# Second-layer attention scores: two matmuls of 128 rows and one of 32 in place of three of 96 rows, and another order of the steps

## Chip, core and metric

The kernel runs on one core of a Trainium2 chip. The metric is the device time of one execution in microseconds. Engines are named as in the profile: PE (matrix multiplication; PEld its weight loads), DVE (vector), ACT (scalar, activations), POOL (general purpose), SP (issues the DMAs).

## What is computed

The reference is a backbone of two layers over 1024 latent tokens and 256 context tokens, in float32. The change lies in the second layer, multi-head latent attention. Each of 16 heads has queries and keys of 64 numbers made by projections ("nope") and 32 with rotary positions, which all heads share on the key side:

```python
def mla_keys_values(kv_a, k_pe, kv_norm, w_kvb, row, col):
    kv = (rms_norm(kv_a, kv_norm) @ w_kvb).reshape(B_, L, C_HEADS, C_NOPE + C_V)
    k_nope, v = kv[..., :C_NOPE], kv[..., C_NOPE:]
    k = jnp.concatenate([k_nope, jnp.broadcast_to(k_pe, (B_, L, C_HEADS, C_ROPE))], axis=-1)

def one(qblk):
    s = jnp.einsum('bqhd,bkhd->bhqk', qblk, k).astype(jnp.float32) * scale
    p = jax.nn.softmax(s, axis=-1).astype(v.dtype)
    return jnp.einsum('bhqk,bkhd->bqhd', p, v)
```

The queries are the 1024 latent tokens; the keys are all 1280 tokens.

## The kernel before, in words

Float32 products that need accuracy are made from two parts: a "high" part, the number rounded to the matmul's float32r format, and a "low" part, the rest. A product is the sum of high x high, high x low and low x high; `mm3` (L98) issues the three for the projections, and the function `scores` (L1201) does so for the scores. `hi` (L85) makes a high part by a cast, `lo` (L94) a low part by a subtraction.

`layer1_attention` (L1174) walks over 64 units: 8 pairs of heads, 4 groups of 256 queries, 2 heads. A unit has 256 queries of one head, as two blocks j of 128 queries, against 1280 keys. PSUM has eight banks: `s0` and `s1` take two each (the scores of a block j against 1024 keys), `sx` one (both blocks against the 256 context keys), `tm` has two buffers of one bank that transposes and projections take in turn, and `acc` one. `s0`, `s1` and `sx` have one buffer: the next unit's scores wait until the exponents have read them.

Inside `manual_schedule` the order of the instructions of PE, ACT, DVE and POOL is the order of the program, and that is written out by hand in `ORDER1` (L43), a list of steps that every unit n goes through:

- S0 S1 (block 0, keys 0 to 511 and 512 to 1023), S2 S3 (block 1), S4 (both blocks, context keys): `scores` on PE.
- X0 X1 X2: `maxima` on DVE; P0 P1: `peak`, a small DVE operation on them; E0 E1 (1024 keys) and E2 E3 (256): `exponent` on ACT.
- T0 to T4: `turn`, four transposes each of the previous unit's probabilities on PE and a copy out of `tm`, on the engine that `TURNS` (L45) names for each (V is DVE, A is ACT). T0 T1 are of block 0, T2 T3 of block 1, T4 of the context keys.
- A0: `av`, the product with the values, half of a pair of units' in each unit. I, U, C: the sums' inverses, their spreading (U is two PE transposes in odd units) and the gating of a finished pair.
- B and R: `prep_q`, in even units, the queries of the group that the unit after next starts with. B is the projection on PE, R what follows: casts and subtractions into `qh` and `ql`, with the rotary part loaded from DRAM by SP into `pe` and put into rows 64 to 95.
- D and L: a step each of `prep_v` ("value step") or `prep_pair` ("key step"), by `VALUES` and `PAIR` (L41). A key step's D is a projection on PE into a `tm` bank (512, 512 and 256 keys for a pair), its L two ACT casts and two DVE subtractions, one of each for a head, that empty that bank into `kring`.

`kring` holds the keys of the present pair of heads and the next; `kpe` (L1086) puts the rotary keys into its rows 64 to 95. SP has no order of its own by hand: its DMAs stand in the scheduler's order and are issued in turn.

The code that the change touches:

Of the kernel before, what the change touches and what calls it, by code (L numbers as in the profile page):

```python
# [41 lines left out]
WQ = 'VGG'  # L42
ORDER1 = 'S0 S1 T0 T1 I C X0 S4 S2 X2 P0 T2 T3 E0 E2 S3 T4 D X1 P1 L E3 E1 A0 U B R'.split()  # L43
AVS = ((0, 5),), ((5, 10),)
TURNS = 'VAAVA'  # L45
KPE = {3: [0], 5: [1]}
KPEE = "AV"
ORDER0 = 'S0 S1 D Q M S2 S3 A1 D D A2 P HV HG S4 U D A3 X I F'.split()
# [5 lines left out]
class Kernel:  # L54
# [887 lines left out]
    def layer1_in(self):  # L942
# [6 lines left out]
        self.kvl = lp.tile([P, T], F32R, name="kvl")  # L949
        self.pk = lp.tile([P, T], F32, name="pk")  # L950
        qn = lp.tile([P, 2], F32, name="qn")
        kn = lp.tile([P, 1], F32, name="kn")
        gp = self.pool(self.es_h1, "g1", bufs=2, side="right")
        es_r = ExitStack()
        rp = self.pool(es_r, "r1", bufs=2, side="right")
# [129 lines left out]

    def kpe(self, par, heads=range(2)):  # L1086

        for e in heads:
            kh, kl = self.kring[par][e]
            if par == 0:  # L1090
                self.hi("A", kh[64:96], self.pk[64:96])
                self.lo("V", kl[64:96], self.pk[64:96], kh[64:96])
            else:
                for to, v in zip((kh, kl), self.kring[0][e]):
                    self.hi(KPEE[to is kl], to[64:96], v[64:96].bitcast(F32))

# [32 lines left out]
    def prep_pair(self, hp):  # L1129
# [9 lines left out]
        for g0, gn in GROUPS:  # L1139
            ps = self.project(w, self.split(kvh, kvl), g0, gn)  # L1140
            yield
            c = slice(g0, g0 + gn)
            src = [ps[64 * e:64 * e + 64] for e in range(2)]
            for e in range(2):
                nc.scalar.copy(ring[e][0][0:64, c], src[e])
            for e in range(2):
                nc.vector.tensor_tensor(ring[e][1][0:64, c], src[e], ring[e][0][0:64, c].bitcast(F32), op=ALU.subtract)
            yield

    def prep_q(self, hp, qg):  # L1150

        nc = self.nc
        pool = self.qpool[qg % len(self.qpool)]
        cols = slice(qg * self.QG, (qg + 1) * self.QG)
        pe = self.t(self.c1, [P, 2, self.QG], F32, "pe", bufs=2)
        nc.sync.dma_start(pe[64:96], self.pe_d[64 * hp:64 * hp + 64, cols].rearrange("(e p) c -> p e c", e=2))
        tp = self.bank()
        w = self.wq[hp]
        for k in range(2):
            self.mm3(tp[:, 0:self.QG], *w[k], self.qnh[:, k, cols], self.qnl[:, k, cols], k == 0, k == 1)  # L1160
        yield
        qh = self.t(pool, [P, 2, self.QG], F32R, "qh", bufs=1)
        ql = self.t(pool, [P, 2, self.QG], F32R, "ql", bufs=1)
        src = [tp[64 * e:64 * e + 64, 0:self.QG] for e in range(2)]
        for e in range(2):
            nc.scalar.copy(qh[0:64, e], src[e])  # L1166
        for e in range(2):
            nc.vector.tensor_tensor(ql[0:64, e], src[e], qh[0:64, e].bitcast(F32), op=ALU.subtract)  # L1168
        self.hi("A", qh[64:96], pe[64:96])
        self.lo(WQ[2], ql[64:96], pe[64:96], qh[64:96])  # L1170
        self.pq[(hp, qg)] = [(qh[:, e], ql[:, e]) for e in range(2)]
        yield

    def layer1_attention(self):  # L1174
# [98 lines left out]
        def inverses(m):  # L1273

            t = totals.pop(m)
            nc.vector.tensor_tensor(t[:, 2], t[:, 0], t[:, 1], op=ALU.add)
            spread[m] = v = self.t(c2, [P, 2, 2, 64], F32, "spread", bufs=2)
            nc.vector.reciprocal(t[:, 2], t[:, 2])
# [43 lines left out]
        with self.tc.manual_schedule(engines={E.PE, E.Activation, E.DVE, E.Pool}):  # L1322
            for n in range(N + 3):
                odd = n % 2
                for op in ORDER1:
                    o, a = op[0], int(op[1:] or 0)
                    if o in "SXPE":
                        if n < N:
                            {"S": scores, "X": maxima, "P": peak, "E": exponent}[o](n, a)
                    elif o == "T":  # L1330
                        if 1 <= n <= N:
# [247 lines left out]
```

## Time and profile before

| | |
|---|---|
| runs | median 1504.61 us of 3 (1503.4 to 1506.65) |
| profiled execution | its own time 1504.3 us, its span 1502.5 us |
| PE busy | 1439.6 us, 96% of the span |
| DVE, ACT, POOL busy | 879.5, 735.9, 397.4 us |
| granted PE clock | 0.994 of full speed |
| first score matmul of the second layer | starts at 805.6 us |
| last unit's first score matmul | starts at 1389.4 us |

The span runs from the first to the last instruction. "Busy" is time in which an engine has an instruction under way; consecutive matmuls overlap in these records, so their durations add up to more than their share of the time, and the distance between starts tells the pace.

### The profile page before, as it was taken

What the parts mean: (1) busy time and instruction counts of PE and PEld (TensorE: products, weight loads), DVE (VectorE), ACT (ScalarE), POOL (GpSimd) and SP (SyncE); (2) the same over time, 40 slices, a digit from 0 to 9 for tenths busy, and PEclk for the clock granted to TensorE, in tenths of its full rate; (3) what the DMA queues carried; (4) which work ended last, traced back from release to release, by engine and by line L of the source; (5) the groups of instructions that cost most, each with busy time, mean ns of one, the idle gap of its engine ahead of it and who ended that gap; (6) DMA issues with size and microseconds to landing.
All of it is one profiled execution on the core that took longest, in us unless ns stands there. A gap on an engine that the chain in (4) does not pass through costs nothing.

```text
span 1502.5 us, 23133 instructions
## 1 busy us (share of the span) xinstructions
PE 1439.6 (96%) x8849; PEld 1132.6 (75%) x8849; DVE 879.5 (59%) x1690; ACT 735.9 (49%) x1563; POOL 397.4 (26%) x351
## 2 busy tenths in 40 slices
PE   5999999999999799999998999999999999999998
PEld 3766899777666478879887777777777777776786
DVE  5582124356667877543745766676667666766454
ACT  4422310145567635443435766666666666676321
POOL 4243233223556533232470110011001100124100
PEclk9999999999999999999999999999999999999999
DMA  8557401222214646321231000000000000212241
GB/s 329 230 219 272 136 29 29 85 81 85 72 39 155 188 123 191 130 76 57 71 127 39 24 24 15 25 24 24 15 25 24 24 15 22 71 46 81 96 144 71
DMA packets 83783, 132.64 MB, mean 88 GB/s; under 512 B 7552, under 2 KB 59976, under 8 KB 80600
## 3 DMA queue, kind: packets, MB, share of 16 engines
q1 hardware_dynamic: 83528, 130.91, 25.9%
q8 instruction: 69, 1.13, 0.3%
q14 instruction: 42, 0.34, 0.1%
q10 hardware_dynamic: 144, 0.26, 0.0%
HBM read 99.59 MB, written 31.56 MB: 87 GB/s over the span
## 4 chain that ended last, share of the span: by engine, by line
PE 75%; DVE 9%; ACT 5%; issue 4%; DMA 4%; POOL 2%; SPq 0%; POOLq 0%; DVEq 0%; ACTq 0%
PE acc L1270 9%; PE tm L1252 7%; PE s L100 7%; PE s L101 7%; PE s L102 7%; PE b L100 5%; PE b L101 4%; PE b L102 4%; PE s L1215 3%; PE s L1216 3%; PE s L1217 3%; PE tm L100 2%; PE acc L774 2%; DVE peak L1227 2%; ACT prob L1242 2%
## 5 line engine op out<-in xcount | busy, mean ns | idle before, releaser
L1259 ACT COPY pt<-tm 128x512 f32<-128x512 f32 x192 | 112.4, 585 | 165.7 <-PE tm L1252 165.7
L1252 PE MATMUL tm<-ident,prob 128*128 128x128 f32 x1280 | 178.3, 273 | 7.8 <-ACT pt L1259 2.1
L1252 PEld LDWEIGHTS tm<-ident,prob 128*128 128x128 f32 x1280 | 150.8, 140 | 42.0 <-PE tm L1252 9.5
L1242 ACT ACTIVATE prob<-s,peak 128x1024 f32<-128x1024 f32 x128 | 143.3, 1120 | 38.0 <-DVE peak L1231 29.6
L1227 DVE TENSOR_REDUCE peak<-s 128x1 f32<-128x1024 f32 x128 | 155.0, 1211 | 1.8 <-PE s L1217 1.7
L1270 PE MATMUL acc<-pt,v 128*64 128x256 f32 x1280 | 152.0, 384 | 0.0
L96 POOL TENSOR_TENSOR ql<-pe,qh 32x512 fp32r<-32x512 f32 x32 | 40.7, 1271 | 413.2 <-ACT qh L88 386.2
L1261 DVE COPY pt<-tm 128x512 f32<-128x512 f32 x128 | 87.8, 686 | 79.4 <-PE tm L1252 77.4
L96 POOL TENSOR_TENSOR w_lo<-raw,w_hi 128x512 fp32r<-128x512 f32 (+1 forms) x60 | 74.9, 1261 | 199.0 <-DVE w_hi L90 98.5
L1270 PEld LDWEIGHTS acc<-pt,v 128*64 128x64 f32 x1280 | 86.3, 136 | 49.7 <-issue 9.6
L1215 PE MATMUL s<-kh,qh 96*128 96x512 f32 x256 | 109.2, 426 | 2.5 <-DVE raw L186 1.5
L1216 PE MATMUL s<-kl,qh 96*128 96x512 f32 x256 | 100.9, 394 | 0.0
L1217 PE MATMUL s<-kh,ql 96*128 96x512 f32 x256 | 100.8, 394 | 0.0
L1168 DVE TENSOR_TENSOR ql<-tm,qh 64x256 fp32r<-64x256 f32 x62 | 26.1, 421 | 83.7 <-ACT qh L1166 83.3
L100 PE MATMUL b<-h,yh 128*128 128x512 f32 x160 | 63.8, 399 | 3.7 <-ACT yh L88 2.7
L100 PE MATMUL s<-h,w_hi 128*128 128x512 f32 x160 | 63.9, 412 | 2.2 <-ACT qk L380 2.2
L101 PE MATMUL s<-h,w_hi 128*128 128x512 f32 x160 | 63.7, 398 | 0.3 <-DVE rs_v L125 0.3
L101 PE MATMUL b<-h,yh 128*128 128x512 f32 x160 | 63.3, 395 | 0.0
L102 PE MATMUL s<-h,w_lo 128*128 128x512 f32 x160 | 63.0, 395 | 0.0
L102 PE MATMUL b<-h,yl 128*128 128x512 f32 x160 | 62.5, 391 | 0.0
L1242 ACT ACTIVATE prob<-sx,peak 128x256 f32<-128x256 f32 x128 | 61.0, 477 | 0.6
L1217 PEld LDWEIGHTS s<-kh,ql 96*128 96x128 f32 x256 | 48.0, 188 | 11.2
(469 smaller groups left out, 3733.7 us busy)
## 6 DMA issues: line engine op xcount, KB each, us to landing
wa<-in_w_ada_dram SPq DMA_DIRECT2D x16, 1024.0 KB, 9.1
x<-in_xs_dram SPq DMA_DIRECT2D x20, 512.0 KB, 5.6
raw<-in_w_dram SPq DMA_DIRECT2D x17, 512.0 KB, 3.6
wa<-in_w_adag_dram SPq DMA_DIRECT2D x8, 1024.0 KB, 5.9
raw<-in_w_out_dram SPq DMA_DIRECT2D x10, 512.0 KB, 3.9
yf<-y_d SPq DMA_DIRECT2D x10, 512.0 KB, 5.6
x_d<-x SPq DMA_DIRECT2D x8, 512.0 KB, 4.5
raw<-in_w1g_dram SPq DMA_DIRECT2D x8, 512.0 KB, 3.4
```

Of the source, the lines that this page charges most:

```text
L96: e.tensor_tensor(lo, src, hi.bitcast(F32), op=ALU.subtract)
L100: mm(out, lhsT=ah, rhs=bh, start=start, stop=False)
L101: mm(out, lhsT=ah, rhs=bl, start=False, stop=False)
L102: mm(out, lhsT=al, rhs=bh, start=False, stop=stop)
L1215: mm(o, lhsT=qh[0:96, q], rhs=kh[0:96, k0:k1], start=True, stop=False)
L1216: mm(o, lhsT=qh[0:96, q], rhs=kl[0:96, k0:k1], start=False, stop=False)
L1217: mm(o, lhsT=ql[0:96, q], rhs=kh[0:96, k0:k1], start=False, stop=True)
L1227: nc.vector.reduce_max(m[:, 0, a:a + 1], banks[n, a], axis=AX.X)
L1242: nc.scalar.activation(probs[n][j][:, TL:T] if c else probs[n][j][:, 0:TL], src, AF.Exp, bias=peaks[n][:, 2, j:j + 1], scale=scale, accum_ ...
L1252: nc.tensor.transpose(tp[:, o * P:(o + 1) * P], probs[n][j][:, k * P:(k + 1) * P], self.ident)
L1259: nc.scalar.copy(dst, src)
L1270: mm(accs[m][64 * e:64 * e + 64, 0:QG], lhsT=self.v4[hp // 2][:, kt, vc:vc + 64], rhs=pts[2 * m + e][:, kt], start=kt == 0, stop=kt == NT - 1)
```

## The change

Scores: the third matmul of each bank of 512 keys goes. The operands are packed anew so that two matmuls have 128 rows: `qa` holds high and low nope queries (64 + 64 rows) against the high nope keys, which now stand in `ka` twice; `qb` holds the high nope queries, the high rotary queries and the low rotary queries against the low nope keys and the high rotary keys twice. What is left is high rotary queries x low rotary keys, 32 rows. `qc` and `kc` hold these four times over, in rows 0, 32, 64 and 96, and `rotary` (step K) issues one matmul of 32 rows for each of the four banks of `s0` and `s1`, each from another group of 32 rows. For S4 a third matmul of 128 rows stays, with `kz`, in which the three spare copies are multiplied by 0.

The order: S2, S3 and K move ahead of X0; D and L move behind the products; B moves ahead of them; R stands right after E2. T3's copy goes to ACT and T4's to DVE. Copies and casts: `prep_pair` casts each high part twice, `prep_q` loads `pe` with four DMAs in place of one and gives POOL four operations in place of one (`WQ[2]` was G: POOL), `kpe` changes accordingly. `pe` and `spread` have one buffer in place of two, and `pk` moves to another pool.

```diff
-ORDER1 = 'S0 S1 T0 T1 I C X0 S4 S2 X2 P0 T2 T3 E0 E2 S3 T4 D X1 P1 L E3 E1 A0 U B R'.split()
+ORDER1 = 'S0 S1 T0 T1 I C S2 S3 K X0 T2 S4 T3 X2 P0 E0 B X1 P1 E2 R A0 E1 T4 D E3 U L'.split()
-TURNS = 'VAAVA'
+TURNS = 'VAAAV'
...
+        self.kc = k1.tile([P, T], F32R, name="kc")
+        self.kz = k1.tile([P, TC], F32R, name="kz")
...
+        first = self.kring[0][0][1]
         for e in heads:
-            kh, kl = self.kring[par][e]
-            if par == 0:
-                self.hi("A", kh[64:96], self.pk[64:96])
-                self.lo("V", kl[64:96], self.pk[64:96], kh[64:96])
-            else:
-                for to, v in zip((kh, kl), self.kring[0][e]):
-                    self.hi(KPEE[to is kl], to[64:96], v[64:96].bitcast(F32))
+            kb = self.kring[par][e][1]
+            if par or e:
+                self.hi("A", kb[64:128], first[64:128].bitcast(F32))
+                continue
+            for r in (64, 96):
+                self.hi("A", kb[r:r + 32], self.pk[64:96])
+            self.lo("V", self.kc[64:96], self.pk[64:96], kb[64:96])
+            for r in (0, 32, 96):
+                self.nc.vector.tensor_copy(self.kc[r:r + 32], self.kc[64:96].bitcast(F32))
...
             for e in range(2):
-                nc.scalar.copy(ring[e][0][0:64, c], src[e])
+                for r in (0, 64):
+                    nc.scalar.copy(ring[e][0][r:r + 64, c], src[e])
...
-        pe = self.t(self.c1, [P, 2, self.QG], F32, "pe", bufs=2)
-        nc.sync.dma_start(pe[64:96], self.pe_d[64 * hp:64 * hp + 64, cols].rearrange("(e p) c -> p e c", e=2))
+        pe = self.t(self.c1, [P, 2, self.QG], F32, "pe", bufs=1)
+        for r in range(0, P, 32):
+            nc.sync.dma_start(pe[r:r + 32], self.pe_d[64 * hp:64 * hp + 64, cols].rearrange("(e p) c -> p e c", e=2))
...
         for e in range(2):
-            nc.scalar.copy(qh[0:64, e], src[e])
+            nc.scalar.copy(qa[0:64, e], src[e])
         for e in range(2):
-            nc.vector.tensor_tensor(ql[0:64, e], src[e], qh[0:64, e].bitcast(F32), op=ALU.subtract)
-        self.hi("A", qh[64:96], pe[64:96])
-        self.lo(WQ[2], ql[64:96], pe[64:96], qh[64:96])
+            nc.vector.tensor_tensor(qa[64:128, e], src[e], qa[0:64, e].bitcast(F32), op=ALU.subtract)
+        self.hi("G", qc, pe)
+        self.lo("G", qb[96:128], pe[96:128], qc[96:128])
+        self.hi("G", qb[64:96], pe[64:96])
+        self.hi("G", qb[0:64], qa[0:64].bitcast(F32))
...
-                mm(o, lhsT=qh[0:96, q], rhs=kh[0:96, k0:k1], start=True, stop=False)
-                mm(o, lhsT=qh[0:96, q], rhs=kl[0:96, k0:k1], start=False, stop=False)
-                mm(o, lhsT=ql[0:96, q], rhs=kh[0:96, k0:k1], start=False, stop=True)
+                mm(o, lhsT=qa[:, q], rhs=ka[:, k0:k1], start=True, stop=False)
+                mm(o, lhsT=qb[:, q], rhs=kb[:, k0:k1], start=False, stop=False)
+                if a == 4:
+                    mm(o, lhsT=qc[:, q], rhs=self.kz, start=False, stop=True)
+
+        def rotary(n):
+            hp, qg, e = units[n]
+            qc = self.pq[(hp, qg)][e][2]
+            for g in range(4):
+                j, h = divmod(g, 2)
+                r = slice(32 * g, 32 * g + 32)
+                mm(banks[n, j][:, h * 512:(h + 1) * 512], lhsT=qc[r, j * P:(j + 1) * P],
+                   rhs=self.kc[r, h * 512:(h + 1) * 512], start=False, stop=True)
```

Three places of the order, all in the same odd unit, one with a key step. PE from the end of S1 on, before: S1, T0 T1 (each row of four transposes), S4 (its first row), S2, T2 T3. The numbers behind names tell tiles apart; rows of the changed kernel have its own line numbers.

```order
L1215 MATMUL s0_1346_8180<-kh11_7346,qh_1305_7974 128x512
L1216 MATMUL s0_1346_8180<-kl11_7347,qh_1305_7974 128x512
L1217 MATMUL s0_1346_8180<-kh11_7346,ql_1306_7975 128x512
L1252 MATMUL tm_1348_8188<-ident_69,prob_1331_8122 128x128 x4
L1252 MATMUL tm_1349_8194<-ident_69,prob_1331_8122 128x128 x4
L1215 MATMUL sx_1352_8206<-kh11_7346,qh_1305_7974 128x256
...
L1215 MATMUL s1_1353_8213<-kh11_7346,qh_1305_7974 128x512
L1216 MATMUL s1_1353_8213<-kl11_7347,qh_1305_7974 128x512
L1217 MATMUL s1_1353_8213<-kh11_7346,ql_1306_7975 128x512
L1252 MATMUL tm_1354_8219<-ident_69,prob_1332_8123 128x128 x4
L1252 MATMUL tm_1355_8225<-ident_69,prob_1332_8123 128x128 x4
```

The same place with the change: S1, T0 T1, S2 (S3 repeats its rows), K (two rows of two matmuls), T2, S4 (its first two rows), T3.

```order
L1227 MATMUL s0_1353_8234<-kh11_7366,qa_1306_7991 128x512
L1228 MATMUL s0_1353_8234<-kl11_7367,qb_1307_7992 128x512
L1275 MATMUL tm_1355_8240<-ident_69,prob_1337_8173 128x128 x4
L1275 MATMUL tm_1356_8246<-ident_69,prob_1337_8173 128x128 x4
L1227 MATMUL s1_1358_8256<-kh11_7366,qa_1306_7991 128x512
L1228 MATMUL s1_1358_8256<-kl11_7367,qb_1307_7992 128x512
...
L1239 MATMUL s0_1353_8234<-kc_7095,qc_1308_7993 128x512 x2
L1239 MATMUL s1_1358_8256<-kc_7095,qc_1308_7993 128x512 x2
L1275 MATMUL tm_1360_8267<-ident_69,prob_1338_8174 128x128 x4
L1227 MATMUL sx_1361_8273<-kh11_7366,qa_1306_7991 128x256
L1228 MATMUL sx_1361_8273<-kl11_7367,qb_1307_7992 128x256
...
L1275 MATMUL tm_1362_8280<-ident_69,prob_1338_8174 128x128 x4
```

S2 and S3 with K now stand between T1 and T2, and S4 between T2 and T3; each bank has two rows where it had three.

PE at the end of that unit, before: T4's last transpose, the three matmuls of the key step D (`kvh` and `kvl` with `w_hi` and `w_lo`, into a `tm` bank), the products (twenty records in the trace, ten rows here, one shown), U, and S0 of the next unit.

```order
L1252 MATMUL tm_1358_8238<-ident_69,prob_1332_8123 128x128
L100 MATMUL tm_1359_8244<-kvh_6005,w_hi_1337_8142 128x512
L101 MATMUL tm_1359_8244<-kvl_6006,w_hi_1337_8142 128x512
L102 MATMUL tm_1359_8244<-kvh_6005,w_lo_1338_8143 128x512
L1270 MATMUL acc_1341_8152<-pt_1308_7989,v4_1161_7183 64x256
...
L1285 MATMUL acc_1341_8152<-ident_69,spread_1350_8201 128x128 x2
L1215 MATMUL s0_1360_8268<-kh10_7344,qh_1344_8172 128x512
L1216 MATMUL s0_1360_8268<-kl10_7345,qh_1344_8172 128x512
L1217 MATMUL s0_1360_8268<-kh10_7344,ql_1345_8173 128x512
```

With the change: T4's last transpose, D, U, the next unit's S0 (S1 repeats its rows), T0 and T1, and S2.

```order
L1275 MATMUL tm_1365_8305<-ident_69,prob_1338_8174 128x128
L99 MATMUL tm_1366_8311<-kvh_6005,w_hi_1349_8226 128x512
L100 MATMUL tm_1366_8311<-kvl_6006,w_hi_1349_8226 128x512
L101 MATMUL tm_1366_8311<-kvh_6005,w_lo_1350_8227 128x512
L1308 MATMUL acc_1345_8203<-ident_69,spread_1357_8253 128x128 x2
L1227 MATMUL s0_1367_8324<-kh10_7364,qa_1342_8192 128x512
L1228 MATMUL s0_1367_8324<-kl10_7365,qb_1343_8193 128x512
...
L1275 MATMUL tm_1369_8330<-ident_69,prob_1363_8288 128x128 x4
L1275 MATMUL tm_1370_8336<-ident_69,prob_1363_8288 128x128 x4
L1227 MATMUL s1_1372_8347<-kh10_7364,qa_1342_8192 128x512
```

The products stand no longer between D and the next unit; T1 (`tm_1370`) takes the buffer that D (`tm_1366`) had.

ACT in that unit, before: E0 E2, T4's copy, the key step's two casts, E3 E1, and the next unit's T1 copy.

```order
L1242 ACTIVATE prob_1356_8231,total_1333_8124<-s0_1346_8180,peak_1351_8204 128x1024
L1242 ACTIVATE prob_1356_8231,total_1333_8124<-sx_1352_8206,peak_1351_8204 128x256
L1259 COPY pt_1347_8187<-tm_1358_8238 128x512
L1145 CAST kh00_7091<-tm_1359_8244 64x512
L1145 CAST kh01_7093<-tm_1359_8244 64x512
L1242 ACTIVATE prob_1357_8232,total_1333_8124<-sx_1352_8206,peak_1351_8204 128x256
L1242 ACTIVATE prob_1357_8232,total_1333_8124<-s1_1353_8213,peak_1351_8204 128x1024
L1259 COPY pt_1361_8275<-tm_1363_8282 128x4x128
```

With the change: T2's and T3's copies, E0 E2 E1 E3, the key step's four casts, and the next unit's T1 copy.

```order
L1282 COPY pt_1354_8239<-tm_1360_8267 128x4x128
L1282 COPY pt_1354_8239<-tm_1362_8280 128x4x128
L1265 ACTIVATE prob_1363_8288,total_1339_8175<-s0_1353_8234,peak_1359_8265 128x1024
L1265 ACTIVATE prob_1363_8288,total_1339_8175<-sx_1361_8273,peak_1359_8265 128x256
L1265 ACTIVATE prob_1364_8289,total_1339_8175<-s1_1358_8256,peak_1359_8265 128x1024
L1265 ACTIVATE prob_1364_8289,total_1339_8175<-sx_1361_8273,peak_1359_8265 128x256
L1154 CAST kh00_7091<-tm_1366_8311 64x512 x2
L1154 CAST kh01_7093<-tm_1366_8311 64x512 x2
L1282 COPY pt_1368_8329<-tm_1370_8336 128x4x128
```

The casts stand behind all exponents of the unit, and the copy of T4 is gone from ACT.

## Rows read from the trace of the kernel before

**Rows 1.** Busy time of each engine, 100 us of the attention; columns in its first line.
```profile
core 0: us, PE busy (x) PEld busy (x) DVE busy (x) ACT busy (x) POOL busy (x), PEclk, DMA share, GB/s
...
1000.00:1100.00 100.00, 98.27 (x694) 77.45 (x696) 65.62 (x119) 63.83 (x143) 10.38 (x13) 1.00 0.07 20
```

**Rows 2.** Timeline of PE in three units: start us, us, engine, line, operation, tiles, count.
```profile
890.85 0.49 PE L100 MATMUL tm<-kvh,w_hi 128*128 128x512 f32 x1
891.18 0.39 PE L101 MATMUL tm<-kvl,w_hi 128*128 128x512 f32 x1
891.41 0.40 PE L102 MATMUL tm<-kvh,w_lo 128*128 128x512 f32 x1
891.74 2.38 PE L1270 MATMUL acc<-pt,v 128*64 128x256 f32 x20
894.05 0.44 PE L1285 MATMUL acc<-ident,spread 128*128 128x128 f32 x2
894.24 0.48 PE L1215 MATMUL s<-kh,qh 96*128 96x512 f32 x1
...
895.02 0.39 PE L1215 MATMUL s<-kh,qh 96*128 96x512 f32 x1
895.25 0.40 PE L1216 MATMUL s<-kl,qh 96*128 96x512 f32 x1
...
895.71 1.04 PE L1252 MATMUL tm<-ident,prob 128*128 128x128 f32 x8
896.51 0.36 PE L1215 MATMUL sx<-kh,qh 96*128 96x256 f32 x1
...
905.84 1.35 PE L1252 MATMUL tm<-ident,prob 128*128 128x128 f32 x8
906.95 0.36 PE L1215 MATMUL sx<-kh,qh 96*128 96x256 f32 x1
```

**Rows 3.** Group by line of PE's weight loads: busy us, mean ns | idle before them.
```profile
L1217 PEld LDWEIGHTS s<-kh,ql 96*128 96x128 f32 x256 | 48.0, 188 | 11.2
```

**Rows 4.** Timeline of PE at a sum of the first layer (L779).
```profile
504.83 0.40 PE L708 MATMUL s<-qs,kl 128*128 128x512 f32 x1
505.16 0.64 PE L779 MATMUL acc<-fold,ones 128*32 128x256 f32 x8
505.73 0.51 PE L707 MATMUL s<-qs,kh 128*128 128x512 f32 x1
506.07 0.39 PE L708 MATMUL s<-qs,kl 128*128 128x512 f32 x1
```

**Rows 5.** Who waited for whom, 830 to 1390 us: us in total, times, longest.
```profile
PEld tm L1252 <- PE tm L1252: 9.5, 29, 0.4
...
PEld tm L100 <- DVE pt L1261: 8.7, 16, 0.7
```

**Rows 6.** Timeline of ACT and of DVE at a key step and in the next unit.
```profile
892.30 1.18 ACT L1145 CAST kh<-tm 64x512 fp32r<-64x512 f32 x2
...
899.92 1.12 ACT L1242 ACTIVATE prob<-s,peak 128x1024 f32<-128x1024 f32 x1 [0.71 <-DVE peak L1231]
...
893.51 1.39 DVE L1147 TENSOR_TENSOR kl<-tm,kh 64x512 fp32r<-64x512 f32 x2 [1.34 <-ACT kh L1145]
...
897.75 1.22 DVE L1227 TENSOR_REDUCE peak<-s 128x1 f32<-128x1024 f32 x1
```

**Rows 7.** Timeline of PE around the start of the attention.
```profile
792.93 0.47 PE L100 MATMUL s<-h1h,w_hi 128*128 128x512 f32 x1 [1.05 <-DVE kl L1147]
...
805.56 0.50 PE L1215 MATMUL s<-kh,qh 96*128 96x512 f32 x1 [1.47 <-DVE raw L186]
...
810.74 0.50 PE L1215 MATMUL s<-kh,qh 96*128 96x512 f32 x1 [0.71 <-ACT prob L1242]
```

**Rows 8.** Groups by line of ACT and of POOL: busy us, mean ns | idle before them.
```profile
L88 ACT CAST qh<-pe 32x512 fp32r<-32x512 f32 x32 | 19.7, 615 | 2.4 <-DMA pe<-pe_d 1.6
...
L96 POOL TENSOR_TENSOR ql<-pe,qh 32x512 fp32r<-32x512 f32 x32 | 40.7, 1271 | 413.2 <-ACT qh L88 386.2 <-issue 25.2 <-DMA raw<-in_wq_n_dram 1.7
```

More of the change, by code (lines that the diff above doesn't have):

```diff
@@ L42 @@
 WQ = 'VGG'
-ORDER1 = 'S0 S1 T0 T1 I C X0 S4 S2 X2 P0 T2 T3 E0 E2 S3 T4 D X1 P1 L E3 E1 A0 U B R'.split()
+ORDER1 = 'S0 S1 T0 T1 I C S2 S3 K X0 T2 S4 T3 X2 P0 E0 B X1 P1 E2 R A0 E1 T4 D E3 U L'.split()
 AVS = ((0, 5),), ((5, 10),)
-TURNS = 'VAAVA'
+TURNS = 'VAAAV'
 KPE = {3: [0], 5: [1]}
-KPEE = "AV"
 ORDER0 = 'S0 S1 D Q M S2 S3 A1 D D A2 P HV HG S4 U D A3 X I F'.split()
@@ L949, in layer1_in @@
         self.kvl = lp.tile([P, T], F32R, name="kvl")
-        self.pk = lp.tile([P, T], F32, name="pk")
         qn = lp.tile([P, 2], F32, name="qn")
@@ L953, in layer1_in @@
         gp = self.pool(self.es_h1, "g1", bufs=2, side="right")
+        self.pk = gp.tile([P, T], F32, name="pk", bufs=1)
         es_r = ExitStack()
@@ L1086, in kpe @@
     def kpe(self, par, heads=range(2)):
+        first = self.kring[0][0][1]
         for e in heads:
-            kh, kl = self.kring[par][e]
-            if par == 0:
-                self.hi("A", kh[64:96], self.pk[64:96])
-                self.lo("V", kl[64:96], self.pk[64:96], kh[64:96])
-            else:
-                for to, v in zip((kh, kl), self.kring[0][e]):
-                    self.hi(KPEE[to is kl], to[64:96], v[64:96].bitcast(F32))
+            kb = self.kring[par][e][1]
[7 more added lines that the diff above has]
+                self.nc.vector.tensor_copy(self.kc[r:r + 32], self.kc[64:96].bitcast(F32))
+            row = self.t(self.small, [P, 1], F32, "row", bufs=1)
+            self.nc.vector.reduce_sum(row, self.ident[:, 0:32], axis=AX.X)
+            self.nc.vector.tensor_scalar_mul(self.kz, self.kc[:, TL:T].bitcast(F32), row[:, 0:1])
     def prep_first(self):
@@ L1161, in prep_q @@
         yield
-        qh = self.t(pool, [P, 2, self.QG], F32R, "qh", bufs=1)
-        ql = self.t(pool, [P, 2, self.QG], F32R, "ql", bufs=1)
+        qa, qb, qc = (self.t(pool, [P, 2, self.QG], F32R, tag, bufs=1) for tag in ("qa", "qb", "qc"))
         src = [tp[64 * e:64 * e + 64, 0:self.QG] for e in range(2)]
         for e in range(2):
-            nc.scalar.copy(qh[0:64, e], src[e])
+            nc.scalar.copy(qa[0:64, e], src[e])
         for e in range(2):
-            nc.vector.tensor_tensor(ql[0:64, e], src[e], qh[0:64, e].bitcast(F32), op=ALU.subtract)
-        self.hi("A", qh[64:96], pe[64:96])
-        self.lo(WQ[2], ql[64:96], pe[64:96], qh[64:96])
-        self.pq[(hp, qg)] = [(qh[:, e], ql[:, e]) for e in range(2)]
+            nc.vector.tensor_tensor(qa[64:128, e], src[e], qa[0:64, e].bitcast(F32), op=ALU.subtract)
[3 more added lines that the diff above has]
+        self.hi("G", qb[0:64], qa[0:64].bitcast(F32))
+        self.pq[(hp, qg)] = [(qa[:, e], qb[:, e], qc[:, e]) for e in range(2)]
         yield
@@ L1203, in scores @@
             hp, qg, e = units[n]
-            (qh, ql), (kh, kl) = self.pq[(hp, qg)][e], self.kring[hp % 2][e]
+            (qa, qb, qc), (ka, kb) = self.pq[(hp, qg)][e], self.kring[hp % 2][e]
             if a == 4:
@@ L1276, in inverses @@
             nc.vector.tensor_tensor(t[:, 2], t[:, 0], t[:, 1], op=ALU.add)
-            spread[m] = v = self.t(c2, [P, 2, 2, 64], F32, "spread", bufs=2)
+            spread[m] = v = self.t(c2, [P, 2, 2, 64], F32, "spread", bufs=1)
             nc.vector.reciprocal(t[:, 2], t[:, 2])
@@ L1329, in layer1_attention @@
                             {"S": scores, "X": maxima, "P": peak, "E": exponent}[o](n, a)
+                    elif o == "K":
+                        if n < N:
+                            rotary(n)
                     elif o == "T":
```

## Prediction

> **What bounds the kernel now.** I read the busy time by stretches first, then single units in the timeline, then the list of waits. In 100 us of the second layer's attention PE is busy 98, DVE 66, ACT 64, POOL 10 [rows 1]. So that stage, 64 units from 805.56 us on [rows 7], lasts as long as PE's queue: a microsecond leaves the program when PE does less, or when PE no longer waits.
>
> PE's pace is read from starts. A score matmul over 512 keys starts 0.23 us after the one before it (895.02, 895.25), six of them take 1.47 us (894.24 to 895.71), eight transposes 0.80 (895.71 to 896.51), the twenty records of a unit's products 2.31 (891.74 to 894.05) [rows 2]. The duration shown, 0.39 us, is longer than the pace because matmuls overlap; only the pace counts.
>
> **The change, part by part.** *Scores.* Each of the four banks of 512 keys had three matmuls of 96 rows and now has two of 128 rows. Rows do not set the pace: the 128-row matmuls of the key projection (891.18, 891.41) stand 0.23 us apart as the 96-row scores do [rows 2]. The third part is left to four matmuls of 32 rows, one in each row group. Removed: 4 x 0.2325 (between 0.23 and 1.47 / 6) = 0.93 us a unit, 64 x 0.93 = **59.5 us**. The two halves over the 256 context keys keep three matmuls each: no change.
>
> *The four 32-row matmuls (K).* No row of this trace uses a part of the array's rows. The nearest is the sum of the first layer, which uses a quarter of its columns: eight records for four column groups, 256 columns each, weights of 32 columns [rows 4]. It takes 0.57 us (505.16 to 505.73). The products, two column groups side by side, need 0.23 us for a round of the same length (2.31 for ten); two rounds of four would be 0.46, so four groups do run side by side, and 0.11 us is lost. The matmul ahead takes 0.33 us in place of 0.23, the one behind 0.34: another 0.21. One visit to a divided array so costs 0.32 us on top of its stream. For K that is one round of 512 columns, 0.23, and 0.32, and 0.05 more by my choice, as its weights have 128 columns in place of 32: **0.60 us**, 64 x 0.60 = **38.4 us**. The bounds are 0.23 (no price for the visit) and 4 x 0.23 + 0.37 = 1.29 (the groups run one after another); 0.60 is what the nearest row gives. The Trainium skill, TensorEngine Tiling (Array Packing), Key Properties, has a rule that speaks against this edit: changing the tiling mode drains the engine. The 0.32 us of [rows 4] agrees for columns; no run here shows it for rows.
>
> *Waits of PE that go.* In the window from 830 to 1390 us PE's weight loads waited 9.5 us in 29 places for the transposes' own queue, and 8.7 us in 16 places for a DVE copy [rows 5]. The first is T1 in every odd unit: the pair T0 T1 takes 1.11 us there (905.84 to 906.95) against 0.80 [rows 2], because the query projection B stood right ahead of S0 and its bank was still being read. B now stands ahead of the products, and its bank is wanted again only after them. The second is a value step D after T4, whose bank T3 had left: the T3 copy waited on DVE behind the peaks. T3's copy is now ACT's, and comes ahead of the exponents. Of the 18.2 us, 19.5 over 64 units, I keep 1.5 for units with both B and D: **-18 us**.
>
> *A wait that comes.* The key steps of a pair change places: D stood ahead of the products, and the casts and subtractions L that free its bank had the products, U, six scores and T0 (2.31 + 0.19 + 1.47 + 0.40 = 4.4 us) to run under. Now D is PE's last work of a unit but U, and T1 of the next unit takes the very bank. Cover: U 0.19, four scores 1.01, T0 0.40 = 1.6 us. Needed after D's last matmul: 0.2 to the first cast, four casts in place of two at some 0.6 us each (892.30, 1.18 for two), of which the third has to end (1.2 + 0.58) before the second subtraction (0.69: 1.39 for two) [rows 6], and 0.1 back to PE: 2.8 us. T1 waits 1.2 us, in 7 pairs x 2 steps of 512 keys = 17 us; the third step, of 256, waits about 0.4, 7 x 0.4 = 3. Together **+20 us**. Behind T1 nothing adds: DVE's T0 copy stands behind the same subtractions, and S2 S3 K give it 1.6 us before T2 needs its bank.
>
> *The start.* In the first unit the peaks now wait for eight scores and K, 8 x 0.2325 + 0.60 = 2.46 us, in place of six, 1.47; the next unit's S0, which stood at 810.74 after 0.71 us of waiting for the exponent that follows them [rows 7], comes 1.0 us later. The doubled casts before the attention lengthen the 1.05 us wait at 792.93 [rows 7] by one cast, 0.6. Together **+1.6 us**.
>
> *At nothing.* The peaks X0 wait for K, some 3.5 us into a unit. From X0's start to E0's pass 2.2 us (897.75 to 899.92), and E0 takes 1.12 [rows 6]: by 7 us the banks of S0 and S1 are free, and the next S0 comes after 8.5. E1 ends another 2 us later (E2, two query casts, E1), and the S2 that needs its banks comes 1.8 us after S0. The cover is some 1 us at least; if PE waits elsewhere it grows. ACT gets 14 x 2 x 0.6 + 7 x 2 x 0.4 = 22 us of second casts and loses 32 x 0.615 = 20 us of rotary casts [rows 8]. POOL takes three more operations for a query group (one of it 1.27 us now [rows 8]; at as much each the four end 5.1 us after the query casts, and the unit that needs them starts 8 us later). SP issues four loads in place of one for a group; with one buffer each waits for POOL's reads, and the gate loads and stores stand behind it, but DMA's share is 7% there [rows 1] and each has a unit or more of time. The rotary copies for the keys run on DVE and ACT under the gate projections.
>
> **Sum**, against the profiled execution's own 1504.3 us (0.3 below the median of the runs): 1504.3 - 59.5 + 38.4 - 18 + 20 + 1.6 = 1486.8, so **1487 us**. With K between 0.5 and 0.75 and the wait of key steps 2 us either way, its own range is 1478 to 1498. The point at which nothing is gained is K = 0.87 us.
>
> **The rivals.** *No price for the visit.* If entering and leaving row groups costs nothing, K is one round, 0.23 us, and the time 1486.8 - 64 x 0.37 = 1463. For it: the price in [rows 4] was seen on column groups alone, and a turn between transposes and matmuls costs 0.10 us at most (890.85 to 891.18 is 0.33) [rows 2]. Against it: [rows 4] is the only divided array that can be read. By the Trainium skill, TensorE: Matmul & The Clock Gate, Measured speedup vs the span model, four row tiles take one matmul and about 4 ns for each further tile; by that the sum would be 1463 too, an estimate. No row here shows it. Chance 15%.
>
> *The weights come one after another.* Four loads of 128 columns replace loads that hid under matmuls of 0.23 us. If each holds the next group back by 0.10 us, the pace of transposes that each bring their own weights (0.80 for eight), K is 0.60 + 3 x 0.10 = 0.90 and the time 1506; at the 0.19 us that such a load is shown to take [rows 3] it is 1.17 and 1524. I take the first, since loads overlap there. Chance 10%.
>
> *Not packed at all.* If the four do not run side by side, K is 1.29 us and the time 1486.8 + 64 x 0.69 = 1531: slower than before, and the change does not do what it says. It turns at K = 0.87. For it: the four are issued in a row into four banks, and no row shows two row groups at once. Against it: column groups do it in [rows 4]. Chance 10%.
>
> *The order costs more than I count.* ACT becomes late: E3 and the casts end after T1's turn, the stall of the key steps spreads to values steps and to the even units, 10 to 20 us more, 1497 to 1507. For it: ACT's work is now bunched behind E0; against it, it is busy only 64% [rows 1]. Chance 10%.
>
> **How the numbers follow.** The forecast has 55%. The range 1462 to 1510 holds it, the fourth rival, most of the first and the lower end of the second, about 82%. A measurement of this kernel can tell 0.2%, 3 us, from no change. Faster than 1501.6: 55 + 15 + half of the fourth = 75%. Within 0.2%: the other half of the fourth and half of the second, 10%. Slower: the rest of the second, and the third, 15%.
>
> **What would show it.** In the new trace the four 32-row matmuls should start within some 0.05 us of each other, and from the last score ahead of them to T2 should pass 0.23 + 0.60 us; starts 0.23 us apart would prove the third rival, 0.1 us apart the second, and 0.45 in all the first. T1 after a key step should be late by 1.2 us, 14 times, with the DVE subtraction as releaser; the 0.3 us in odd units and the wait of value steps should be gone. If PE's idle time in the attention exceeds 30 us, or units without a key step are not shorter by 0.3 us than before, my account is wrong.

## The result, and the profile after

The changed kernel takes 1545.33 us (median of 4 runs, 1542.2 to 1547.68) against 1504.01 us for the kernel before on the same chip: 1.0269 times as long, 95% interval 1.0257 to 1.0281. The forecast was 1487 us with a range of 1462 to 1510: wrong in its sign. One execution, of experiment 6, ran for 4812.86 us and is left out below.

The profiled execution, the fastest of the four, has a span of 1540.3 us, 37.8 longer. Its granted PE clock is 0.984, before 0.994. I split the span at two score matmuls, the first of unit 0 and the first of unit 63, and call what lies between them the stage:

| us | before | after | difference |
|---|---|---|---|
| start to the first score | 805.6 | 808.8 | +3.2 |
| the stage, 63 units | 583.8 | 616.7 | +32.9 |
| the rest | 113.1 | 114.8 | +1.7 |

The same view as [rows 1], 100 us of the attention (busy us of each engine, granted clock, DMA share, GB/s):

```profile
core 0: us, PE busy (x) PEld busy (x) DVE busy (x) ACT busy (x) POOL busy (x), PEclk, DMA share, GB/s
1000.00:1100.00 100.00, 86.81 (x602) 64.47 (x601) 59.84 (x104) 60.30 (x132) 15.29 (x22) 0.95 0.09 27
```

PE is busy 87 in place of 98, and no other engine fills up: PE waits. [rows 5] has waits of the weight loads (PEld). The rows of the matmuls (PE) say how long PE itself stood still, and for what, over the same 830 to 1390 us (us in total, times, longest):

```profile
PE tm L1275 <- DVE kl L1156: 44.9, 21, 2.6
PE tm L99 <- DVE qa L1177: 7.1, 16, 0.5
```

The 21 waits are T1's, one behind each key step (7 pairs x 3), 44.9 us in all. The longest row of the matmuls before was that of D behind T4:

```profile
PE tm L100 <- DVE pt L1261: 4.9, 16, 0.4
```

So D in even units waited 4.9 us before, for T3's copy, and waits 7.1 us now, for the query bank. T1's old wait in odd units, the first row of [rows 5], is gone.

One key step on PE, from the last score ahead of K on (columns: start us, us, engine, line, operation, tiles, shape, count, [idle before it <- releaser]):

```profile
992.95 0.39 PE L1228 MATMUL s<-kl,qb 128*128 128x512 f32 x1
993.26 0.51 PE L1239 MATMUL s<-kc,qc 32*128 32x512 f32 x4
993.70 0.66 PE L1275 MATMUL tm<-ident,prob 128*128 128x128 f32 x4
994.12 0.37 PE L1227 MATMUL sx<-kh,qa 128*128 128x256 f32 x1
...
998.72 0.39 PE L101 MATMUL tm<-kvh,w_lo 128*128 128x512 f32 x1
998.95 0.38 PE L1308 MATMUL acc<-ident,spread 128*128 128x128 f32 x2
999.09 0.48 PE L1227 MATMUL s<-kh,qa 128*128 128x512 f32 x1
...
1000.10 0.60 PE L1275 MATMUL tm<-ident,prob 128*128 128x128 f32 x4
1003.17 0.83 PE L1275 MATMUL tm<-ident,prob 128*128 128x128 f32 x4 [2.47 <-DVE kl L1156]
1003.65 0.77 PE L1227 MATMUL s<-kh,qa 128*128 128x512 f32 x1
1004.22 0.63 PE L1228 MATMUL s<-kl,qb 128*128 128x512 f32 x1
1004.65 0.63 PE L1227 MATMUL s<-kh,qa 128*128 128x512 f32 x1
1005.07 0.63 PE L1228 MATMUL s<-kl,qb 128*128 128x512 f32 x1
```

K is what was forecast, or a little less: four matmuls in one row, the last score 0.31 us ahead, T2 0.44 us behind; 0.75 us from that score to T2 where 0.83 was said. The four start within 0.01 us of each other. T2 itself takes 0.42 us to S4, where T3, which does not follow K, takes 0.35 (1007.80 to 1008.15). What follows D is not what was forecast. D's last matmul starts at 998.72. T1 comes at 1003.17 after 2.47 us of waiting, and the scores behind it stand 0.43 us apart (1004.65 to 1005.07), not 0.23. ACT and DVE over the same stretch:

```profile
999.15 0.21 ACT L1265 ACTIVATION_READ_ACCUMULATOR prob<-sx,peak 128x1 f32 x1
999.25 2.35 ACT L1154 CAST kh<-tm 64x512 fp32r<-64x512 f32 x4
...
1001.63 1.39 DVE L1156 TENSOR_TENSOR kl<-tm,kh 64x512 fp32r<-64x512 f32 x2 [2.49 <-ACT kh L1154]
1003.05 0.69 DVE L1284 COPY pt<-tm 128x512 f32<-128x512 f32 x1
```

The first subtraction starts when the fourth cast has ended (999.25 + 2.35 = 1001.60), and T1 when the second subtraction has. The trace also holds what each instruction signals: in all 21 key steps only the last of the four casts raises the semaphore for which the first subtraction waits (it starts 0.03 us behind that cast), and only the second subtraction raises the one for which T1 waits. And the granted clock in stretches of 2 us of PE:

```profile
core 0: us, PE busy (x), PEclk, DMA share, GB/s
1001.00:1003.00 2.00, 0.00 (x0) 1.00 0.00 0
1003.00:1005.00 2.00, 1.83 (x7) 0.61 0.03 8
1005.00:1007.00 2.00, 2.00 (x11) 0.53 0.20 66
1007.00:1009.00 2.00, 2.00 (x19) 1.00 0.22 66
```

PE does nothing from 1001 to 1003, and then runs for some 4 us mostly at the lower of its two levels, 1.2 in place of 2.4 GHz. Such a unit takes 14.1 us, one of the same kind whose wait was as long but kept the clock 12.6. Of the 14 waits behind steps of 512 keys, 8 were followed by the low clock; these units are 1.3 to 1.5 us longer than those of their kind, 11.6 us in all.

### The profile page after: what moved, and what is told of

Its sections match the earlier page's. It is cut to its first block, busy times and chain, and to the rows that moved or that the text cites. A ratio compares the mean times of both kernels' runs of the same rounds, so it can differ in the third digit from the quotient of the medians.

```text
span 1540.3 us, 23388 instructions
## 1 busy us (share of the span) xinstructions
PE 1428.8 (93%) x8849; PEld 1103.3 (72%) x8849; DVE 890.1 (58%) x1692; ACT 748.5 (49%) x1580; POOL 454.2 (29%) x447
## 4 chain that ended last, share of the span: by engine, by line
PE 41%; ACT 11%; DVE 4%; issue 4%; DMA 2%; POOL 1%; SPq 0%; DVEq 0%; POOLq 0%; ACTq 0%
PE tm L1275 9%; ACT prob L1265 5%; PE acc L1293 4%; PE s L99 3%; PE s L100 3%; PE s L101 3%; PE s L1227 3%; PE s L1228 3%; ACT kh L1154 3%; PE s L1239 2%; ACT pt L1282 1%; PE b L99 1%; PE b L101 1%; PE b L100 1%; DVE kl L1156 1%
## 5 line engine op out<-in xcount | busy, mean ns | idle before, releaser
L1275 PE MATMUL tm<-ident,prob 128*128 128x128 f32 x1280 | 197.2, 283 | 46.6 <-DVE kl L1156 44.9
L1275 PEld LDWEIGHTS tm<-ident,prob 128*128 128x128 f32 x1280 | 145.6, 142 | 102.0 <-issue 75.0
L1265 ACT ACTIVATE prob<-s,peak 128x1024 f32<-128x1024 f32 x128 | 142.7, 1114 | 12.6 <-DVE peak L1254 10.4
L1227 PE MATMUL s<-kh,qa 128*128 128x512 f32 x256 | 114.3, 447 | 5.9 <-ACT prob L1265 4.5
L91 POOL CAST qb<-qa 64x512 fp32r<-64x512 f32 x32 | 19.5, 608 | 319.7 <-ACT qa L1175 319.7
L1228 PE MATMUL s<-kl,qb 128*128 128x512 f32 x256 | 104.4, 408 | 0.0
L1227 PEld LDWEIGHTS s<-kh,qa 128*128 128x128 f32 x256 | 50.0, 195 | 13.6 <-ACT prob L1265 5.4
L1228 PEld LDWEIGHTS s<-kl,qb 128*128 128x128 f32 x256 | 50.4, 197 | 6.4
L745 DVE TENSOR_TENSOR pt<-pt,tm 128x512 f32<-128x512 f32 x68 | 42.4, 682 | 21.8 <-ACT mb L736 18.9
```

What stands on the lines that cost most here:

```text
L1227: mm(o, lhsT=qa[:, q], rhs=ka[:, k0:k1], start=True, stop=False)
L1228: mm(o, lhsT=qb[:, q], rhs=kb[:, k0:k1], start=False, stop=False)
L1265: nc.scalar.activation(probs[n][j][:, TL:T] if c else probs[n][j][:, 0:TL], src, AF.Exp, bias=peaks[n][:, 2, j:j + 1], scale=scale, accum_ ...
L1275: nc.tensor.transpose(tp[:, o * P:(o + 1) * P], probs[n][j][:, k * P:(k + 1) * P], self.ident)
```

## The experiments

**Theory A**: the packing gains about what was forecast, and the loss is the wait of T1 for the key step's bank and the low clock that follows. **Rivals**: B, the packing itself (K, the doubled copies) costs it; C, the order costs it, with late peaks and exponents. Each time below stands beside runs of the kernel before on the same chip in the same batch. "Stage" is the stretch of the table above, in the profiled execution.

**1. The second copy on POOL.** Frees the bank 1.2 us earlier.

```diff
-                for r in (0, 64):
-                    nc.scalar.copy(ring[e][0][r:r + 64, c], src[e])
+                nc.scalar.copy(ring[e][0][0:64, c], src[e])
...
+            for e in range(2):
+                self.hi("G", ring[e][0][64:128, c], ring[e][0][0:64, c].bitcast(F32))
```

> Edit: the key step's second copy (rows 64 to 127 of each key tile) is made by POOL from the first copy in memory, after the subtractions; ACT makes two casts of a key group in place of four. Theory A (the loss sits in the turn T1 that waits for the key step's bank, and in the half clock that follows): the bank is free 1.2 us earlier, so the row 'PE tm turn <- DVE kl' falls from 45 us to about 20 to 25 (14 x 1.2 + 7 x .6 less), the half clock becomes rarer, and the time is 1503 to 1522. Rival B (the packing itself, K and the extra copies, costs): POOL now has more to do and K is unchanged, so 1540 to 1550. Rival C (the order of scores and maxima costs): unchanged as well, 1540 to 1550.

Measured: 1508.65 us (1.0026, interval 1.0017 to 1.0035), clock 0.994. The wait:

```profile
PE tm L1276 <- DVE kl L1155: 23.4, 21, 1.4
```

The wait fell by 21.5 us, the stage by 34.0 (616.7 to 582.7). POOL had 42 copies more to make, K was the same: B and C fall as the main cause. 12.5 us more came back than were waited.

**2. D and L earlier.** `... E2 R D L A0 E1 T4 E3 U` at the end of the list.

> Edit: in the list of a unit D (first half of a value or key step) goes from behind T4 to ahead of A0, and L (its second half) from the end to behind D, so that the 2.3 us of products, T4 and two scores lie between the key step's matmuls and the turn that needs its bank. Theory A: the 45 us of waits and most of the half clock go, 1472 to 1492. Rival B (packing itself costs): waits move or go, but at most the 45 us named in the waits come back, 1498 to 1515. Rival C (the order costs because peaks and exponents come late): the new place of L puts four casts ahead of the exponent E1, so later still: 1530 to 1550.

Measured: 1511.89 us (1.0048, 1.0033 to 1.0063). A miss: 33 us better than the change, 20 above A's range and inside that of B. The row leaves B no need: T1's wait had become one of T0, and 21.0 of its 44.9 us were still there (what the packing is worth, 13 settles):

```profile
PE tm L1275 <- DVE kl L1156: 21.0, 21, 1.4
```

**3. Both edits.**

> Both edits: the second copy on POOL, and D and L ahead of A0. Theory A: no wait for the key step is left and the clock is back at .99 to 1.00: 1466 to 1484, at most 8 us under the kernel with the second edit alone. Rival B: 1498 to 1515. Rival C: 1520 to 1550.

Measured: 1487.81 us (0.9888, 0.9873 to 0.9903): 3.8 above A's range, 10 under B's and 32 under C's. Its ACT shows why D's new place gave less than its cover:

```profile
1037.86 1.11 ACT L1266 ACTIVATE prob<-s,peak 128x1024 f32<-128x1024 f32 x1
...
1039.42 1.18 ACT L1153 CAST kh<-tm 64x512 fp32r<-64x512 f32 x2
1040.62 1.12 ACT L1266 ACTIVATE prob<-s,peak 128x1024 f32<-128x1024 f32 x1
```

D is done by 1037.85, but L stood behind E0 and E2 on ACT, so the bank waited 1.6 us for its first cast. Earlier on PE is not earlier on ACT.

**4. The order alone**: the kernel before, unpacked, with `ORDER1` of the change without K, and its `TURNS`.

> Edit: the kernel before, with its three 96-row matmuls per score and its tiles and copies, under the changed kernel's list (without K) and its table of who copies which turn. It has the new order and none of the packing. Theory A: the key step has two casts, so its bank takes 3.0 us, and the scores in front of T1 are .46 us longer, cover 2.1: a wait of about .9 us x 14, some 11 us for value steps behind R, less the 18 us of old waits: 1500 to 1520. Rival B (packing costs): 1495 to 1510. Rival C (the order costs as it stands): 1540 to 1575.

Measured: 1515.82 us (1.0076, 1.0059 to 1.0092), in A's range. The order costs 11 us by itself, with 14.6 us of waits at T1 (21 times, up to 1.1 us). C is no more than a part; the change with its packing is 30 us slower still.

**5. R, D and L ahead of E2**, on top of 3: `... B X1 P1 R D L E2 A0 E1 T4 E3 U`.

> Edit: the kernel with both edits (second copy on POOL, D and L ahead of A0), and in its list R, D and L stand ahead of the exponent E2 instead of behind it, so ACT casts a step's bank .67 us earlier. In the kernel with both edits some 5 us per 16 units are above the product time, in units that follow a step, as short waits of transposes for DVE and ACT (kl, kh, qa, pt). Theory A (what is left are those short waits for the step's bank): 3 to 8 us less than 1487.8, so 1479 to 1485. Rival C (exponents late cost more than step banks): E2 and E1 come later, so 1488 to 1496.

Measured: 1477.86 us (0.982, 0.9802 to 0.9837), 1 us better than A's range.

**6. T1 behind K**, nothing else: `S0 S1 T0 I C S2 S3 K X0 T1 T2 S4 T3 ...`.

> Edit: the changed kernel with one move in its list: T1 (the turn that waits for the key step's bank) goes behind S2 S3 and K, to stand beside T2. D, L and the four casts stay. The cover between D and T1 grows from 1.6 to 3.05 us. Theory A: waits of T1 fall from 2.6 us to about 1.2 (512 columns) and to 0 to .2 (256 columns), about 17 us in all against 45, the clock comes back to .99, as in the kernel with the second copy on POOL: 1498 to 1512. Rival B (the copies themselves cost): four casts are still made, so 1535 to 1548. Rival D (the clock falls for another reason than the wait): the waits go but clock stays at .984: 1515 to 1530.

> The changed kernel with T1 behind K, once more for its trace (its time was 1516, where 1498 to 1512 was expected). Theory A: T1 still waits for the key step's bank, by more than the 1.2 us expected, and the granted clock is .99; the wait row of T1 on DVE kl then stands at 20 to 30 us. Rival: that row is at 17 us or less and the rest is a wait of T2 or T3 for the copies of T0 and T1, which now stand close together.

Measured: 1516.08 us (three executions; 1.0079, 1.0062 to 1.0096), and 1513.55 in the one that left the trace, a miss by 2 to 4 us. T1's wait is the forecast one, and the clock is 0.991:

```profile
PE tm L1275 <- DVE kl L1156: 16.0, 14, 1.2
PE tm L99 <- DVE qa L1177: 12.7, 16, 0.8
PE s L99 <- ACT s L1506: 3.6, 1, 3.6
```

The surplus is elsewhere: D waits 5.6 us more for the query bank than in experiment 1, and the first output projection 3.6 us. The time lies in the range of rival D, but the clock came back, so D falls. Of the two answers offered for the trace the rival had the row right (17 us or less), but not where the rest lies.

**7. K twice in one visit**, on top of 3: eight matmuls in a row in place of four (`for v in range(8): g = v % 4`).

> Edit: the kernel with both edits, but K makes its four matmuls in row groups twice in a row (eight in one visit, the rotary rows counted twice, so the scores are not the reference's). It prices K in place, 64 times. Theory A as read from the trace (a visit costs about .30 us once, and each set of four .23): 64 x .23 = 15 us more than 1487.8, so 1499 to 1506. Rival B1 (every set costs the whole .53): 34 us more, 1518 to 1526. Rival B2 (the four do not run beside each other, .9 a set): 1540 to 1550.

Measured: 1507.99 us, 20.2 more than 3 and 2 above A's range. The stage grew by 14.3 (562.3 to 576.6), which is 0.227 a unit; the rest lies ahead of it and behind. The profile of one visit:

```profile
994.86 0.40 PE L1229 MATMUL s<-kl,qb 128*128 128x512 f32 x1
995.19 0.74 PE L1241 MATMUL s<-kc,qc 32*128 32x512 f32 x8
995.86 0.33 PE L1277 MATMUL tm<-ident,prob 128*128 128x128 f32 x1
```

From K to the turn 0.67 us in place of 0.44. A second set of four costs a stream of 0.23; the rest of K, 0.75 - 0.23 - 0.23 = 0.29 us, is paid once a visit. T2, 0.06 us longer behind K than a turn elsewhere, comes on top, so K costs some 0.58 us in all.

**8. Both: T1 behind K on top of 5**, and **11**, the same with the list of 5 for the last unit and the turns behind it.

> Edit: as the kernel with casts ahead of E2, and T1 behind K as well, so K and the maxima come .4 us earlier and no turn stands between S1 and S2 but T0. Theory A: the short waits at T0 and T1 shrink further: 1474 to 1484. Rival C (S2 must then wait for the exponent of the unit before, E1, that reads its bank): 1484 to 1500.

> Edit: the kernel with casts ahead of E2 and T1 behind K, but its last unit and the three turns behind it go by the list of the kernel without T1 behind K. Units of the one with T1 behind K are shorter (140.7 against 141.8 us per 16) but its end, from the last unit's first score, is 6 us longer (a wait of 3.5 us for the activation at the first output tile). Theory A: the shorter units and the shorter end together: 1470 to 1475. Rival: the end is longer for another reason: 1477 to 1481.

Measured: 1479.78 us for the first, with a stage 3.2 us shorter than that of 5 (549.1 against 552.3) and an end 6.3 longer (120.5 against 114.2); 1474.05 us for the second (0.9784, 0.9769 to 0.9799), as A had it. This is the fastest of all with experiment 12, 2.2% under the kernel before. PE has no gap left:

```profile
1000.00:1100.00 100.00, 100.00 (x749) 76.18 (x747) 69.79 (x123) 64.73 (x147) 22.91 (x35) 1.00 0.12 35
```

**9. Work added into the wait.** Nine idle score matmuls (five behind the 256-key step) between T0 and T1, into the bank that S2 overwrites:

```diff
+            for _ in range(FILL[last]):
+                mm(b[:, 0:512], lhsT=qa[:, P:2 * P], rhs=ka[:, 0:512], start=True, stop=True)
```

> Edit: the changed kernel, with work added and nothing taken away. In the 21 units that follow a key step, nine (five behind the 256-column group) idle score matmuls of 128 rows are put between T0 and T1, into the bank that S2 overwrites: 2.1 us (1.15 us) of work in the stretch in which TensorE now waits for the bank. The bank comes free when it did. Theory A (the wait costs its own 45 us, and the half clock that follows it another 15, as the second copy on POOL took 21.5 us of wait and 36.7 us of time): the wait is filled, the clock stays at full speed, and the kernel with more work is faster: 1526 to 1536, granted clock .99. Rival E (the clock falls for another reason, or the 15 us were the copies' own): 1543 to 1552, clock .98.

Measured: 1531.93 us (1.017, 1.0155 to 1.0185): 13.4 us faster than the change, with 161 matmuls more (14 x 9 + 7 x 5). T1 starts 3.3 us behind S1's last row as ever, but PE has worked until 0.4 us before:

```profile
999.98 0.39 PE L1229 MATMUL s<-kl,qb 128*128 128x512 f32 x1
1000.21 0.60 PE L1287 MATMUL tm<-ident,prob 128*128 128x128 f32 x4
1000.56 2.33 PE L1242 MATMUL s<-kh,qa 128*128 128x512 f32 x9
1003.28 0.63 PE L1287 MATMUL tm<-ident,prob 128*128 128x128 f32 x4 [0.38 <-DVE kl L1157]
1003.66 0.48 PE L1228 MATMUL s<-kh,qa 128*128 128x512 f32 x1
1003.98 0.40 PE L1229 MATMUL s<-kl,qb 128*128 128x512 f32 x1
1004.21 0.39 PE L1228 MATMUL s<-kh,qa 128*128 128x512 f32 x1
```

The scores behind it are 0.23 us apart, the units of 14.1 us are gone (12.64 at most), and the stage is 12.5 us shorter (604.2): the very 12.5 of experiment 1. So the low clock costs some 12 us of the stage (12.5 by either experiment, 11.6 counted unit by unit), and it is the idle stretch that brings it, not the work.

**10. The bank copied at once, the order untouched.** Pairs 1 to 7:

```diff
+                raw = self.t(self.rawp, [P, D], F32, "raw", bufs=2)[:, 0:gn]
+                nc.scalar.copy(raw, ps)
+                for e in range(2):
+                    kh, own, other = ring[e][0], slice(64 * e, 64 * e + 64), slice(64 - 64 * e, 128 - 64 * e)
+                    self.hi("G", kh[own, c], raw[own])
+                    self.lo("G", ring[e][1][0:64, c], raw[own], kh[own, c])
+                    self.hi("G", kh[other, c], kh[own, c].bitcast(F32))
```

> Edit: the changed kernel with its list as it is; only the way in which a key step leaves its bank is new (pairs 1 to 7). ACT copies the whole bank to memory in one instruction (.6 us), and POOL makes both copies of the high part and the low part from there, six instructions. The bank is held for about 1.0 us in place of 4.2, under the cover of 1.6. Theory A: no wait at T1, clock .99 to 1.00, the order stays: 1474 to 1488. Rival B (the packing's copies cost, wherever they are made) or a POOL that slows VectorE: 1490 to 1505. Rival C (order): over 1505.

Measured: 1482.98 us (0.9841, 0.9824 to 0.9858). One edit at one place takes 62 us off the change. ACT copies at 985.38, and T0 and T1 stand in one row without a wait:

```profile
985.38 0.60 ACT L1153 COPY raw<-tm 128x512 f32<-128x512 f32 x1
```

```profile
986.01 0.39 PE L1238 MATMUL s<-kl,qb 128*128 128x512 f32 x1
986.24 1.03 PE L1285 MATMUL tm<-ident,prob 128*128 128x128 f32 x8
987.03 0.48 PE L1237 MATMUL s<-kh,qa 128*128 128x512 f32 x1
```

**12. The same bank copy on top of 11.**

> Edit: as the kernel with its own list for the end, and the bank of a key step copied to memory in one instruction, all splitting on POOL (pairs 1 to 7). ACT has .6 us less and VectorE 1.4 us less to do in a key step. Theory A (about 1.3 us of short waits per 16 units are left): 1465 to 1472. Rival (POOL slows VectorE, or its late copies hold up the first scores of a new pair): 1473 to 1482.

Measured: 1473.88 us (0.9784, 0.977 to 0.9799), as 11: a miss by 2 us, in the rival's range. But no new wait made up for a gain: the stage takes 548.8 us, that of 11 548.7. Where PE has no gap, less work for ACT and DVE buys nothing.

**13. Experiment 10 without the packing**: 4 with the bank copy.

> Edit: the kernel before under the changed kernel's list (without K), three 96-row matmuls a score, and the key step's bank copied to memory at once and split by POOL (pairs 1 to 7). Beside the changed kernel with the same bank copy (1483.0 us), the packing is the only difference. Theory A (a unit's four scores cost 1.86 us packed behind one visit of K of .53, and 2.79 us unpacked: .33 to .4 us a unit): 1483 + 64 x .33 to .4, so 1503 to 1510. Rival B (the packing's gain is eaten by K and copies): 1480 to 1492. Rival (all .93 us of a unit count, the visit is hidden): 1535 to 1545.

Measured: 1498.76 us (0.9967, 0.9954 to 0.9979), 4 us under A's range. Its stage is 575.8 us, that of 10 is 555.5: the packing is worth 20.3 us. The total differs by 15.8 only, because unit 0 starts 4.5 us earlier in 13 (807.0 against 811.5). The two ran on different chips; against the kernel before on its own chip they are 1.26% apart, 19 us.

## Why the prediction was wrong, point by point

The stage can be put together step by step, each step one kernel against another:

| step | kernels | forecast us | measured us |
|---|---|---|---|
| new order, key step's bank copied at once | before to 13 | -18 | -8.0 |
| packing and K | 13 to 10 | -21.1 | -20.3 |
| key step's bank held by four casts and two subtractions | 10 to after | +20 | +61.2 |
| sum | | -19.1 | +32.9 |

**Scores and K: right.** 59.5 - 38.4 = 21.1 us were forecast; 20.3 came (0.32 of 63 units). K was put at 0.60 us and costs 0.58: 0.23 of stream, 0.29 for the visit (experiment 7) and 0.06 at the turn behind it. The 0.32 read from column groups in [rows 4] so held for row groups; the 0.05 added for the wider weights was a guess, and it happens to be about what the turn behind K costs. The first three rivals, "no price for the visit", "one after another" and "not packed", fall with K's 0.75 us to T2 and its four starts within 0.01 us (the upper case of the second adds up to 1523, not 1524). The rule of the Trainium skill, TensorEngine Tiling (Array Packing), Key Properties, that changing the tiling mode drains the engine, agrees with the 0.29 us. By the span model of the Trainium skill (TensorE: Matmul & The Clock Gate, Measured speedup vs the span model) K would take some 0.24 us, an estimate; the starts and the 0.23 us of a second set agree with it, but it has no term for the visit, and the measurement, 0.52 to T2 (0.23 and 0.29), decides.

**"A wait that comes": the step that failed.** It said that T1 waits 1.2 us behind a step of 512 keys, because the second subtraction needs the third cast: 2.8 us needed, 1.6 covered. The row shows 2.47 us, and 1.4 behind a step of 256 keys where 0.4 was said. Needed were 0.3 us to the first cast (U follows D at 998.95, the cast comes at 999.25, behind E3), 2.35 for all four casts, 1.39 for both subtractions and 0.15 back: 4.2 us, of which 1.7 were covered. The trace of before had said it: in [rows 6] two casts start at 892.30 and take 1.18 us, and the first of the two subtractions starts at 893.51, after both. I assumed an overlap of casts and subtractions that the row excludes: in none of the 21 key steps of that trace does a subtraction start before both casts have ended. With the waits as measured the term would have been 45 us and the forecast 1512. What keeps them apart is the program's own signal, raised by the last cast alone; why the scheduler sets one signal for the batch, no run tells. The Trainium skill, PSUM — Partial Sum Buffer (PSUM bank collisions raise a hardware error), says that software must keep ACT and DVE from reading the same rows of one bank at the same time; the trace agrees (no such reads overlap) and goes further, as the first subtraction, of rows 0 to 63, waits for the casts of rows 64 to 127 too.

**What the forecast had no term for: the low clock.** A wait of 2.5 us costs more than itself: in 8 of 14 cases PE then ran for some 4 us mostly at the lower level, some 12 us in all (experiments 1 and 9). It was not in the sum. The Trainium skill, TensorE: Matmul & The Clock Gate (What's actually happening), tells of a clock that falls to half when PE idles; the trace agrees, with 0.53 behind idle stretches of 2.5 us. Of the 61.2 us, 44.9 are the waits' row and some 12 the clock; about 4 stay unassigned.

**Waits that go: half right.** T1's wait in odd units went, and had its right price: T0 and T1 take 1.10 us there before and 0.79 in 13, 31 units x 0.31 = 9.6 us. The wait of D in even units did not go. The forecast took its 8.7 us from the weight loads [rows 5]; the matmuls had waited 4.9, and now wait for R's casts and subtractions, 6.8 us in 13 and 7.1 in the change, where 1.5 was kept for all. 9.6 less and some 2 more are about the -8.0 of the table.

**The fourth rival**, an ACT that comes late to the casts, is not the cause: the first cast starts 0.3 us behind D, 0.2 was forecast, and no turn behind a value step waits.

**The start**: S0 came 3.2 us later in this profile, +1.6 was forecast. Over the kernels with the packing it lies between 807.0 and 811.5, so I draw nothing from the difference. Unit 0 itself takes 6.1 us in place of 5.2, about the forecast 1.0 more.

**At nothing**: held. X0 waits 50 us for K in all (the row of DVE), and no matmul waits for an exponent behind it except four first scores at the stage's two ends (4.5 us, before 1.0); POOL's and SP's new work shows in no wait of PE.

Of the signs named in the prediction's last part, PE's idle time above 30 us was the one that came true (52 us in the two rows of waits), while units in which PE does no step's work and waits for none became 0.48 us (even, 8.98 to 8.50) and 0.51 us (odd, 8.56 to 8.05) shorter, as it said.

## What to carry to other kernels

When an edit moves the step that fills a shared buffer towards the next user of that buffer, write down the whole chain that empties it, from rows of the very chain and with every instruction in series until a row shows two side by side. The largest cure by one edit here was to shorten the hold (one copy out, split later on an idle engine: 62 us); moves in the list alone gave 29 to 33, and the two fastest kernels have a shorter hold and moves in the list. And price a stall of the matrix engine of a few microseconds higher than its length: here 8 of 14 stalls of 2.5 us cost some 1.5 us more.

## What was not expected of the hardware

- Idle work can make a program faster: 161 matmuls put into waits took 13.4 us off, because PE's granted clock stayed at 1.00 where it had been 0.53 to 0.61 behind waits of 2.5 us. Behind the waits of 1.3 to 1.4 us of experiment 1 it stayed at 1.00 too. Why 6 of 14 equal waits kept the clock is open.
- Four matmuls in four row groups start together and cost 0.23 us for 512 columns, and a visit costs 0.29 us on top, whether one set is issued or two, and 0.06 us at the turn behind it.
